# Two fp32 networks on one core: projections that end by token tiles, a reordered mixer, and two more places for experts' weights

## The chip, the cores and the metric

One core of a Trainium2 chip runs the whole program in one launch. The metric is device time in microseconds, from the first to the last instruction and what little lies around them, as the median of several runs. Lower is better.

## The reference

256 tokens of 1024 channels pass through two networks, all in fp32. The first has a mixer with dilated-window attention and a gated MLP, a layer of 16 experts, a mixer with two kinds of dense attention, a second layer of 16 experts, and a final norm. The second has four gated feed-forward stages, and between them a mixer of sliding-window attention beside a gated convolution with 31 taps, and a recurrent mixer. What the change touches, cut down:

```
for i in range(2):                               # first network
    x = x + mixer(rmsnorm(x, norm_mix[i]))       # ends with  cat @ w_out
    x = x + ec_moe(rmsnorm(x, norm_ffn[i]))

def ec_moe(h, w_router, w_gate, w_up, w_down):   # each expert takes its 32 best tokens
    aff = softmax(h @ w_router)
    gates, idx = top_k(aff.T, 32)
    y = (silu(h[idx] @ w_gate) * (h[idx] @ w_up)) @ w_down
    return scatter_add(idx, y * gates)

def attn_conv_mixer(h):                          # second network, "even2"
    q, k, v, a, b = split(h @ w_in)
    attn = sliding_window_attention(q, k, v, sinks, rel_bias)
    c = silu(layernorm(causal_conv31(a * sigmoid(b))))
    return concat([attn, c]) @ w_out
```

## The kernel before

`x` stays in SBUF as two tiles of 128 tokens by 1024 channels (t = 0, 1). A product of the mixers and the feed-forward stages is made of three fp32r matmuls (`mm3`): high by high, low by high and high by low part (lines 435 to 437). The parts of a weight piece come from `split`: ScalarE writes `whi` (line 423), VectorE or GpSimd subtracts it and writes `wlo` (line 424). There are seven pairs of `whi` and `wlo`. The activations' parts are `hThi` and `hTlo`, those of a mixer's output `chi` and `clo`.

**Weights.** All large loads are issued on SP's queue in program order, in pieces of 1 MB (128 partitions by 2048), into a ring of six slots (line 393). The experts' weights are used as raw fp32 (lines 1305 and 1359). A layer has 64 pieces for gate and up (`bg`, `bu`) and 32 for down (`by`). Where each piece goes is told by a string, `PLAN`: `r` is a ring slot, `s` a pair of `whi` and `wlo`, `l` and `h` the space of `hTlo` and `hThi`, and a digit is a named place of 8 KB per partition. The first `AHEAD` pieces of a layer can be loaded during the mixer ahead of it (`early`, lines 1200 and 1210); the rest follow as TensorE gives space back (`more`). `grow` opens the places, some at the mixer's start (`feed`) and some at the layer's. Pieces behind the string's end go through the ring.

**The projection at the end of the first network's mixers.** `out_proj(late=True)` multiplies `chi`, `clo` by the output weights. The last rows of the sum are taken in four quarters of 256 columns (`mm4`, `last4`): each quarter ends with the addition to `x`, four transposes (`xTq`), the norm's gain on the way out of PSUM (`hTw`, lines 476 and 478), the squares for the norm, and one quarter later the router's matmuls for those channels (`lg`, line 1157). The layer of experts then forms the norm's factor from the running sum of squares and makes the softmax and the top 32.

**The even mixer of the second network.** `gated` makes the convolution's two inputs (`ba`), `taps` and `spectrum` its transform (`hw`, `sp`) and the products `yw` (lines 1638 to 1642), then six `pf` groups make q, k and v from pieces of 1024 columns. `scores` and `softmax` follow (lines 703 to 728), `back` transforms the convolution back (`yt`) and normalises it, `silu` transposes it (`ty`) and writes `sy`, whose parts are the last four rows of `chi`. `gqa_T` transposes the probabilities (`pt`), `pv` multiplies them by v (`po`). The output projection takes the rows of `chi` in the order 4, 5, 6, 7, 0, 1, 2, 3 (`acc`).

Each engine runs its instructions in the order in which they stand in its queue. Within that order the program, its pools and its priorities decide.

Of the kernel before, what the change touches and what calls it, by code (L numbers as in the profile page):

```python
# [9 lines left out]
F32 = mybir.dt.float32  # L10
F32R = mybir.dt.float32r
AF = mybir.ActivationFunctionType
ALU = mybir.AluOpType
# [3 lines left out]
P = 128  # L17
# [17 lines left out]
PLAN = "7ssslhrrrrrr012ssss3456" "7ssslhrrrrrrssss456"  # L35
AHEAD = 23
# [276 lines left out]
class Core:  # L313
# [170 lines left out]

    def squares(self, n):
# [6 lines left out]
    def running(self, sums, ss, n, eng=None):  # L492

        if n:
            (eng or self.nc.gpsimd).tensor_tensor(sums, ss[:, :, 0] if n == 1 else sums, ss[:, :, n], ALU.add)

    def squares4(self, n, eng=None):
# [8 lines left out]
        self.running(self.s2, self.ss, n, eng)  # L506
# [7 lines left out]
    def pow_rstd(self, ss, n, k, eps=EPS, eng=None):  # L514
# [4 lines left out]
        rs = self.wk.tile([P, k], F32, tag=f"rs{k}", name="rs", bufs=4)  # L519
# [78 lines left out]
    def out_proj(self, cat, name, order, eng=None, late=False):  # L598
# [9 lines left out]
        def mm4(i, t, n):  # L608
            k = order[i]

            self.mm3(acc[n][:, t * S:t * S + S], tuple(v[:, k, t * P:t * P + P] for v in cat),
                     tuple(u[:, S * n:S * n + S] for u in parts[i]), i + t == 0, i == KT - 1 and t == 1)

# [5 lines left out]
        def more(n):  # L619
            if not acc and late:  # L620
                acc.extend(self.bank("acc") for n in range(4))
# [5 lines left out]
        def some(m, ahead=0):  # L627
# [3 lines left out]
            for i in range(i0, done[0]):  # L631
                for t in range(NT):
                    for n in range(4 if late else 2):
                        (mm4 if late else mm)(i, t, n)
# [27 lines left out]

        def rest(n):
            raw.extend(self.load(w[:, CHUNK * n:CHUNK * n + CHUNK]))

        return some, last4 if late else last, rest
# [65 lines left out]
    def even1(self, wz, lead):  # L732
        nc, tc, A = self.nc, self.tc, self.A
        with ExitStack() as cx:
# [3 lines left out]
            self.feed(0, "7012", lead)  # L738
# [3 lines left out]
            router = self.router(0, h0)  # L742
# [95 lines left out]
            self.early("12")  # L838
# [1052 lines left out]
```

## Time and profile before

| | |
|---|---|
| median of 3 runs | 1615.41 us (1615.23 to 1615.72) |
| profiled execution | 1610.24 us, its span 1608.5 us |
| granted TensorE clock, mean over the span | 0.961 |
| TensorE busy | 1467.1 us |
| VectorE, ScalarE, GpSimd busy | 793.0, 644.4, 83.8 us |
| read from HBM | 397.29 MB, 248 GB/s over the span |

Stages in the profiled execution, in us from the span's start: first mixer to 126, layer 0 of experts to 345, second mixer to 438, layer 1 of experts to 658, then the second network, with its even mixer from 842 to 957. A window gives each engine's busy time in a stretch, so a stage's own limit is read from its own windows and not from the whole span. The granted clock is a share of 2.4 GHz: 1.00 is that level and 0.50 is 1.2 GHz.

### The profile page before, as it was taken

How to read it: one execution, taken by the hardware profiler on the slowest of the kernel's cores; microseconds unless marked ns; L12 is line 12 of the kernel's file. 1: busy time of each engine (PE TensorE's matmuls, PEld its weight loads, DVE VectorE, ACT ScalarE, POOL GpSimd, SP SyncE). 2: the span in 40 equal slices, each digit the busy share in tenths (PEclk: the TensorE clock that was granted, in tenths of full speed). 3: DMA queues.
4: the chain of work that ended last, by engine and by line, in shares of the span. 5: the costliest groups of instructions: out<-in, count | busy, mean ns of one | idle time of the engine just before them, and what ended most of it. 6: DMA issues, size and time to landing. Idle time of an engine off the chain costs nothing.

```text
span 1608.5 us, 24597 instructions
## 1 busy us (share of the span) xinstructions
PE 1467.1 (91%) x10220; PEld 1155.4 (72%) x10220; DVE 793.0 (49%) x1328; ACT 644.4 (40%) x1042; POOL 83.8 (5%) x108
## 2 busy tenths in 40 slices
PE   9997967888988677799999899999999999999998
PEld 7794303455842145599895679999999999899997
DVE  6753102248421013555454656555765559865554
ACT  5741101148311012444443544444554447754442
POOL 0000000020000001200001410000000000000000
PEclk9998969999989799899999999999999999999999
DMA  9768999994799999856531535555555554555530
GB/s 364 303 247 334 416 419 420 417 386 152 277 389 417 419 414 382 349 181 218 198 131 54 209 108 208 183 185 186 179 184 185 187 186 142 209 181 183 186 130 26
DMA packets 60815, 399.94 MB, mean 249 GB/s; under 512 B 6808, under 2 KB 7200, under 8 KB 17312
## 3 DMA queue, kind: packets, MB, share of 16 engines
q1 hardware_dynamic: 59584, 394.03, 64.6%
q0 software_dynamic: 1120, 4.35, 0.8%
q8 instruction: 80, 1.31, 0.3%
q14 instruction: 31, 0.25, 0.0%
HBM read 397.29 MB, written 1.06 MB: 248 GB/s over the span
## 4 chain that ended last, share of the span: by engine, by line
PE 61%; issue 6%; DMA 5%; DVE 3%; ACT 2%; POOL 0%; POOLq 0%; DVEq 0%; ACTq 0%
PE acc L435 6%; PE acc L437 6%; PE acc L436 6%; PE bg L436 6%; PE bg L435 5%; PE bg L437 5%; PE bu L436 5%; PE bu L437 5%; PE bu L435 5%; DMA w<-in_m_gu_dram 3%; DMA w<-in_m_d_dram 2%; PE by L1359 1%; PE bu L1305 1%; PE bg L1305 1%; PE xs L1288 1%
## 5 line engine op out<-in xcount | busy, mean ns | idle before, releaser
L424 DVE TENSOR_TENSOR wlo<-w,whi 128x1024 fp32r<-128x1024 f32 x349 | 431.1, 1244 | 284.7 <-ACT whi L423 284.3
L423 ACT CAST whi<-w 128x1024 fp32r<-128x1024 f32 x357 | 369.8, 1046 | 461.6 <-PE acc L437 145.4
L435 PE MATMUL bg<-hThi,whi 128*128 128x256 f32 x752 | 212.8, 284 | 2.8 <-ACT hThi L481 2.4
L436 PE MATMUL bg<-hTlo,whi 128*128 128x256 f32 x752 | 211.6, 282 | 4.1 <-DVE hTlo L482 4.1
L437 PE MATMUL bg<-hThi,wlo 128*128 128x256 f32 x752 | 211.5, 281 | 0.0
L436 PE MATMUL bu<-hTlo,whi 128*128 128x256 f32 x656 | 184.4, 281 | 0.0
L437 PE MATMUL bu<-hThi,wlo 128*128 128x256 f32 x656 | 184.3, 281 | 0.0
L435 PE MATMUL bu<-hThi,whi 128*128 128x256 f32 x656 | 184.2, 281 | 0.0
L436 PEld LDWEIGHTS bg<-hTlo,whi 128*128 128x128 f32 x752 | 142.2, 189 | 7.5 <-DVE hTlo L482 5.8
L435 PEld LDWEIGHTS bg<-hThi,whi 128*128 128x128 f32 x752 | 141.8, 189 | 7.0 <-ACT hThi L481 3.9
L435 PE MATMUL acc<-whi,gh 128*128 128x512 f32 x352 | 139.7, 397 | 4.9 <-ACT gh L430 4.9
L437 PEld LDWEIGHTS bg<-hThi,wlo 128*128 128x128 f32 x752 | 142.2, 189 | 0.0
L436 PE MATMUL acc<-wlo,gh 128*128 128x512 f32 x352 | 139.9, 397 | 0.0
L437 PE MATMUL acc<-whi,gl 128*128 128x512 f32 x352 | 139.8, 397 | 0.0
L437 PEld LDWEIGHTS bu<-hThi,wlo 128*128 128x128 f32 x656 | 124.0, 189 | 0.0
L435 PEld LDWEIGHTS bu<-hThi,whi 128*128 128x128 f32 x656 | 124.0, 189 | 0.0
L436 PEld LDWEIGHTS bu<-hTlo,whi 128*128 128x128 f32 x656 | 123.8, 189 | 0.0
L435 PEld LDWEIGHTS acc<-whi,gh 128*128 128x128 f32 x352 | 66.6, 189 | 19.1 <-ACT gh L430 5.1
L437 PEld LDWEIGHTS acc<-whi,gl 128*128 128x128 f32 x352 | 66.4, 189 | 15.9 <-DVE gl L431 0.6
L1359 PE MATMUL by<-w,aT 128*32 128x256 f32 x1024 | 68.1, 391 | 10.4 <-DMA w<-in_m_d_dram 7.2
L436 PEld LDWEIGHTS acc<-wlo,gh 128*128 128x128 f32 x352 | 66.6, 189 | 14.0
L1338 DVE SCALAR_TENSOR_TENSOR hid<-bu,rsl,hid 128x512 f32<-128x512 f32 x8 | 6.0, 750 | 126.2 <-PE bu L1305 118.1
(407 smaller groups left out, 2284.1 us busy)
## 6 DMA issues: line engine op xcount, KB each, us to landing
w<-in_f_gu_dram SPq DMA_DIRECT2D x84, 1024.0 KB, 5.1
w<-in_m_gu_dram SPq DMA_DIRECT2D x68, 1024.0 KB, 13.3
w<-in_m_d_dram SPq DMA_DIRECT2D x64, 1024.0 KB, 11.7
w<-in_f_d_dram SPq DMA_DIRECT2D x40, 1024.0 KB, 5.1
wx<-in_m_gu_dram SPq DMA_DIRECT2D x32, 1024.0 KB, 9.9
wx<-in_m_gu_dram SPq DMA_DIRECT2D x56, 512.0 KB, 6.7
w<-in_e_out_dram SPq DMA_DIRECT2D x8, 1024.0 KB, 5.3
w<-in_o_out_dram SPq DMA_DIRECT2D x8, 1024.0 KB, 5.0
```

Of the source, the lines that this page charges most:

```text
L423: pin(nc.scalar.copy(hi[:, i:n], w[:, o + i:o + n]))
L424: pin((eng or nc.vector).tensor_sub(lo[:, i:n], w[:, o + i:o + n], hi[:, i:n].bitcast(F32)))
L435: mm(out, a[0], b[0], start=start, stop=False)
L436: mm(out, a[0], b[1], start=False, stop=False)
L437: mm(out, a[1], b[0], start=False, stop=stop)
L1288: nc.tensor.matmul(b[:, :n], self.x[:, t, k * P:k * P + P], ohf[:, t, q0 * P:q1 * P], start=t == 0, stop=t == NT - 1)
L1305: nc.tensor.matmul(b[32 * j:32 * j + 32], xs[q][:, k, 32 * j:32 * j + 32], w[j // 2][:, j % 2 * 512:j % 2 * 512 + 512], start=k == 0, stop ...
L1338: nc.vector.scalar_tensor_tensor(a, bu, rsl[:, q:q + 1], a, op0=ALU.mult, op1=ALU.mult)
L1359: nc.tensor.matmul(b[32 * j:32 * j + 32, o:o + S], aT[:, q, f, 32 * j:32 * j + 32], w[i][:, j * S:j * S + S], start=f == 0, stop=f == 3)
```

## The change

The output projections of the first network's mixers end by four tiles of 128 tokens by 512 columns (`tiles`), with the router's matmuls one tile behind. The transposed `x` goes to the router without the gain (`xTt`), and the gain is multiplied into the router's weights once. The squares are taken per tile and added up in `moe`. Two places, 8 and 9, are added: 8 is loaded in the mixers, 9 is opened at the start of a layer. Their space comes from the scratch for DMA descriptors of GpSimd's queue, set to 1 KB per partition, and from small tiles of `moe` that now share space; the load of `back` for the relative bias is cut into four. In the even mixer of the second network the first pair of q, k, v weights is split ahead of the gate, `pf` of piece 0 goes ahead of the transform, and the probabilities of the first tokens are transposed and multiplied by v around the second `back`, ahead of `silu`.

```diff
-PLAN = "7ssslhrrrrrr012ssss3456" "7ssslhrrrrrrssss456"
-AHEAD = 23
+PLAN = "7ssslhrrrrrr012ssss345689" "7ssslhrrrrrrssss45689"
+AHEAD = 25
+SCRATCH = 1024
...
+    def xTt(self, t, n):
+
+        b = self.bank("tp")
+        for k in range(4):
+            o = (4 * n + k) * P
+            self.nc.tensor.transpose(b[:, k * P:k * P + P], self.x[:, t, o:o + P], self.id)
+        bv = b.rearrange("p (k s) -> p k s", k=4)
+        h = self.hT[0][:, 4 * n:4 * n + 4, t * P:t * P + P]
+        self.nc.scalar.copy(h[:, :2], bv[:, :2])
+        self.nc.vector.tensor_copy(h[:, 2:], bv[:, 2:])
...
-        def last4(hook):
-
-            more(KT - len(parts))
-            for n in range(4):
-                for i in range(done[0], KT):
-                    for t in range(NT):
-                        mm4(i, t, n)
-                if n:
-                    hook(n - 1)
-                xs = self.x[:, :, S * n:S * n + S]
-                nc.vector.tensor_tensor(xs, xs, acc[n].rearrange("p (t c) -> p t c", t=NT), ALU.add)
-                self.room()
-                self.xTq(n)
-                self.squares4(n, nc.vector)
-            hook(3)
...
+        def tiles(hook):
+
+            more(KT - len(parts))
+            self.room()
+            self.ss = self.wk.tile([P, NT, 2], F32, tag="ss", name="ss")
+            todo = []
+            for n in range(2):
+                for t in range(NT):
+                    for i in range(done[0], KT):
+                        mm(i, t, n)
+                    if todo:
+                        hook(*todo.pop())
+                    xs = self.x[:, t, n * 512:n * 512 + 512]
+                    nc.vector.tensor_add(xs, xs, acc[t][n])
+                    self.xTt(t, n)
+                    self.square(xs, self.ss[:, t, n:n + 1], 1 - n)
+                    todo.append((t, n))
+            hook(*todo.pop())
...
-            self.feed(0, "7012", lead)
+            self.feed(0, "70128", lead)
...
-            self.early("12")
+            self.early("128")
...
-            self.feed(1, "70", lead)
+            self.feed(1, "708", lead)
...
-            self.early("70sss")
+            self.early("708sss")
...
-    def router(self, l, pool):
+    def router(self, l, pool, gain):
...
+        nc.vector.tensor_tensor(wr, wr, gain[:, :, None].to_broadcast([P, KT, NE]), ALU.mult)
+
+        def step(t, n):
...
-            self.grow("456" if l == 0 else "3456", cx)
+            self.grow("4569" if l == 0 else "34569", cx)
...
-            nc.vector.tensor_scalar(ms, self.s2, 1.0 / D, EPS, op0=ALU.mult, op1=ALU.add)
+            nc.vector.tensor_tensor(ms, self.ss[:, :, 0], self.ss[:, :, 1], ALU.add)
+            nc.vector.tensor_scalar(ms, ms, 1.0 / D, EPS, op0=ALU.mult, op1=ALU.add)
...
+                ws.extend(self.split(self.load(A["e2_in"][0])))
                 rs, _ = self.rstd()
...
-            def qkv(i, ws):
+            def qkv(i):
+                if i == len(ws):
+                    ws.extend(self.split(self.load(A["e2_in"][i // 2])))
...
             gated()
             taps()
+            qkv(0)
             y = spectrum()
-            for i in range(0, 6, 2):
-                ws = self.split(self.load(A["e2_in"][i // 2]))
-                qkv(i, ws)
-                qkv(i + 1, ws)
+            for i in range(1, 6):
+                qkv(i)
...
             p0 = scores(0, 0)
             back(y, 0)
             p1 = scores(1, 0)
+            p0 = self.gqa_T(1, p0)
             back(y, 1)
+            pv(0, p0)
             p1.update(scores(1, 2))
             silu()
-            pv(0, self.gqa_T(1, p0))
             some(3)
...
-                nc.gpsimd.dma_start(back, bass.AP(tensor=d.tensor, offset=d.offset, ap=[[1, P], [384, 8], [1, S]]))
+                for h in range(0, 8, 2):
+                    nc.gpsimd.dma_start(back[:, h:h + 2], bass.AP(tensor=d.tensor, offset=d.offset + 384 * h,
+                                                                  ap=[[1, P], [384, 2], [1, S]]))
...
-    nc = _bacc.Bacc("TRN2", target_bir_lowering=False, num_devices=1)
+    nc = _bacc.Bacc("TRN2", target_bir_lowering=False, num_devices=1, dynamic_dma_scratch_size=SCRATCH)
```

The string decides what SP issues. Its queue around the start of layer 0, before: the eight half pieces of the last `s` pairs, the places that the layer opens, and what follows (`wx` is a piece outside the ring, `w` one in it).

```order
L1200 DMA wx<-in_m_gu_dram 128x1024 x8
L1210 DMA wx<-in_m_gu_dram 128x2048 x4
L1200 DMA wx<-in_m_gu_dram 128x1024 x6
L1210 DMA wx<-in_m_gu_dram 128x2048 x2
L393 DMA w<-in_m_gu_dram 128x2048 x6
L1200 DMA wx<-in_m_gu_dram 128x1024 x8
L1210 DMA wx<-in_m_gu_dram 128x2048 x3
```

And in the changed kernel:

```order
L1208 DMA wx<-in_m_gu_dram 128x1024 x8
L1218 DMA wx<-in_m_gu_dram 128x2048 x5
L1208 DMA wx<-in_m_gu_dram 128x1024 x6
L1218 DMA wx<-in_m_gu_dram 128x2048 x2
L394 DMA w<-in_m_gu_dram 128x2048 x6
L1208 DMA wx<-in_m_gu_dram 128x1024 x8
L1218 DMA wx<-in_m_gu_dram 128x2048 x5
```

One more place is issued at the layer's start (five instead of four), two more in the second turn (five instead of three), and four ring pieces fewer follow. Place 8 stands further ahead, in the first mixer, behind two other places.

VectorE in the even mixer of the second network, from the gate to the second `pf`, before: `glu` is the gate, `yw` and `u` are the transform's products, `qT` the finished queries.

```order
L424 TENSOR_TENSOR wlo<-w,whi 128x1024
L1618 SCALAR_TENSOR_TENSOR glu<-ba,rs,glu 128x512 x2
L402 COPY hw<-hw 96x512 x2
L1638 TENSOR_TENSOR yw<-sp,hw 96x512 x2
L1639 TENSOR_TENSOR u<-sp,hw 96x512 x2
L1640 TENSOR_TENSOR yw<-yw,u 96x512 x2
L1642 TENSOR_TENSOR yw<-sp,hw 96x512 x2
L424 TENSOR_TENSOR wlo<-w,whi 128x1024 x3
L1679 TENSOR_TENSOR qT<-pf,rrow 128x256
L424 TENSOR_TENSOR wlo<-w,whi 128x1024 x2
L1679 TENSOR_TENSOR qT<-pf,rrow 128x256
```

And in the changed kernel:

```order
L425 TENSOR_TENSOR wlo<-w,whi 128x1024 x3
L1629 SCALAR_TENSOR_TENSOR glu<-ba,rs,glu 128x512 x2
L403 COPY hw<-hw 96x512 x2
L1692 TENSOR_TENSOR qT<-pf,rrow 128x256
L1649 TENSOR_TENSOR yw<-sp,hw 96x512 x2
L1650 TENSOR_TENSOR u<-sp,hw 96x512 x2
L1651 TENSOR_TENSOR yw<-yw,u 96x512 x2
L1653 TENSOR_TENSOR yw<-sp,hw 96x512 x2
L425 TENSOR_TENSOR wlo<-w,whi 128x1024
L1692 TENSOR_TENSOR qT<-pf,rrow 128x256
```

Two `wlo` more stand ahead of `glu`, the first `qT` ahead of `yw`, and one `wlo` instead of three behind `yw`.

ScalarE at the end of that mixer's softmax, before: `p` and `st` are the probabilities and their sums, `sy` the silu of the convolution.

```order
L400 COPY p<-pt 128x512
L708 ACTIVATE st<-st 128x2
L718 ACTIVATE p,st<-p,st 128x256 x2
L708 ACTIVATE st<-st 128x2
L718 ACTIVATE p,st<-p,st 128x256
L728 ACTIVATE p<-p,st 128x256
L718 ACTIVATE p,st<-p,st 128x256
L1670 ACT_TABLE_LOAD
L1670 ACTIVATE sy<-ty,pc_e_6580 128x256
L728 ACTIVATE p<-p,st 128x256
L430 CAST chi<-sy 128x256
L1670 ACTIVATE sy<-ty,pc_e_6580 128x256 x2
```

And in the changed kernel:

```order
L431 CAST chi<-po 128x4x128
L1681 ACT_TABLE_LOAD
L1681 ACTIVATE sy<-ty,pc_e_6361 128x256
L715 ACT_TABLE_LOAD
L715 ACTIVATE st<-st 128x2
L725 ACTIVATE p,st<-p,st 128x256 x2
L715 ACTIVATE st<-st 128x2
L725 ACTIVATE p,st<-p,st 128x256
L735 ACTIVATE p<-p,st 128x256
L725 ACTIVATE p,st<-p,st 128x256
L431 CAST chi<-sy 128x256
L1681 ACT_TABLE_LOAD
```

The first `sy` now stands ahead of the last four exps (`p,st<-p,st`), with a table load of its own on either side, and its `chi` behind them.

## Rows read from the trace of the kernel before

**Rows 1.** The page: busy us, share of the span; DMA's tenths in 40 slices.
```profile
PE 1467.1 (91%) x10220; PEld 1155.4 (72%) x10220; DVE 793.0 (49%) x1328; ACT 644.4 (40%) x1042; POOL 83.8 (5%) x108
...
DMA  9768999994799999856531535555555554555530
```

**Rows 2.** Windows of layer 0: from:to, length, each engine's busy us (instructions), PEclk, DMA share, GB/s.
```profile
39.00:45.00 6.00, 5.27 (x39) 4.30 (x38) 5.37 (x20) 5.71 (x7) 0.00 (x0) 1.00 0.21 49
135.00:141.00 6.00, 6.00 (x26) 2.80 (x27) 1.31 (x4) 0.37 (x1) 0.00 (x0) 0.50 0.46 146
141.00:340.00 199.00, 162.27 (x1284) 70.52 (x1282) 28.63 (x55) 26.39 (x51) 3.40 (x5) 0.91 1.01 415
```

**Rows 3.** Chain of waits, 480 to 600 us: start us, us, what.
```profile
499.50 18.76 DMA w<-in_m_gu_dram
...
564.45 13.78 DMA w<-in_m_d_dram
```

**Rows 4.** Windows around layer 1, columns as in group 2.
```profile
385.00:391.00 6.00, 4.83 (x32) 2.61 (x28) 4.58 (x11) 5.64 (x15) 0.00 (x0) 1.00 0.03 11
451.00:454.00 3.00, 3.00 (x28) 1.11 (x24) 0.35 (x1) 0.00 (x0) 0.00 (x0) 0.87 0.69 199
...
605.00:630.00 25.00, 19.98 (x198) 12.91 (x198) 6.32 (x9) 5.42 (x13) 3.60 (x3) 1.00 0.96 390
```

**Rows 5.** Waits of TensorE, 20 to 60 us: us in total, times, longest.
```profile
PE sc L817 <- ACT qkT L807: 0.7, 1, 0.7
```

**Rows 6.** Timeline of SP's queue at the start of layer 0: start us, us, what.
```profile
126.11 13.11 SPq L1210 DMA_DIRECT2D wx<-in_m_gu_dram  x4
```

**Rows 7.** Timeline of TensorE in the even mixer's projections.
```profile
902.44 0.28 PE L436 MATMUL pf<-hTlo,whi 128*128 128x256 f32 x1
902.56 0.28 PE L437 MATMUL pf<-hThi,wlo 128*128 128x256 f32 x1
```

**Rows 8.** Timeline of TensorE, end of the first mixer; idle time and releaser in brackets.
```profile
124.89 1.12 PE L1157 MATMUL lg<-pc_wr,hTw 128*128 128x16 f32 x8 [0.58 <-DVE hTw L478]
```

**Rows 9.** Timeline of TensorE in the even mixer of the second network.
```profile
885.73 0.58 PE L437 MATMUL pf<-hThi,wlo 128*128 128x256 f32 x1 [4.47 <-DVE wlo L424]
...
910.58 3.70 PE L1652 MATMUL yt<-yw,pc_e 96*128 96x512 f32 x8
...
919.17 1.79 PE L1140 MATMUL po<-p,v 128*64 128x512 f32 x2 [2.37 <-DVE p L402]
...
923.87 0.50 PE L435 MATMUL acc<-whi,chi 128*128 128x512 f32 x1 [0.45 <-ACT chi L430]
```

**Rows 10.** Timeline of VectorE there.
```profile
883.27 1.27 DVE L1642 TENSOR_TENSOR yw<-sp,hw 96x512 f32<-96x512 f32 x2
884.47 3.48 DVE L424 TENSOR_TENSOR wlo<-w,whi 128x1024 fp32r<-128x1024 f32 x3
...
890.28 4.56 DVE L424 TENSOR_TENSOR wlo<-w,whi 128x1024 fp32r<-128x1024 f32 x2
...
919.03 0.54 DVE L1658 TENSOR_SCALAR yt<-yt,ls,rs 128x512 f32<-128x512 f32 x1
```

**Rows 11.** Window behind the wait of `pf`, columns as in group 2.
```profile
885.00:888.00 3.00, 2.27 (x10) 2.27 (x11) 2.94 (x3) 0.00 (x0) 0.00 (x0) 0.54 0.75 262
```

**Rows 12.** Timeline of ScalarE there.
```profile
914.04 0.49 ACT L718 ACTIVATE p<-p,st 128x256 f32<-128x256 f32 x1
...
914.53 0.49 ACT L718 ACTIVATE p<-p,st 128x256 f32<-128x256 f32 x1
...
921.27 1.28 ACT L1670 ACT_TABLE_LOAD   x1
922.57 0.56 ACT L1670 ACTIVATE sy<-ty,pc_e 128x256 f32<-128x256 f32 x1
...
923.43 0.39 ACT L430 CAST chi<-sy 128x256 fp32r<-128x256 f32 x1
```

**Rows 13.** DMA issues: name, queue, count, KB each, median us to landing.
```profile
row_fn<-in_row_fn_dram POOLq DMA_DIRECT2D x1, 512.0 KB, 8.8
```

More of the change, by code (lines that the diff above doesn't have):

```diff
@@ L518, in pow_rstd @@
         (eng or nc.vector).tensor_scalar(ms, ss, 1.0 / n, eps, op0=ALU.mult, op1=ALU.add)
-        rs = self.wk.tile([P, k], F32, tag=f"rs{k}", name="rs", bufs=4)
+        rs = self.wk.tile([P, k], F32, tag=f"rs{k}", name="rs", bufs=4 if k == NT else 2)
         nc.gpsimd.tensor_tensor(rs, ms, self.mhalf[:, :k], ALU.pow)
@@ L606, in out_proj @@
         done = [0]
[L608 to L612, printed above, removed]
         def mm(i, t, n):
@@ L619, in more @@
         def more(n):
-            if not acc and late:
-                acc.extend(self.bank("acc") for n in range(4))
             if not acc:
@@ L661, in last @@
                 self.xT(n)
+        def tiles(hook):
[3 more added lines that the diff above has]
+            todo = []
+            for n in range(2):
+                for t in range(NT):
+                    for i in range(done[0], KT):
+                        mm(i, t, n)
+                    if todo:
[6 more added lines that the diff above has]
+            hook(*todo.pop())
         def rest(n):
             raw.extend(self.load(w[:, CHUNK * n:CHUNK * n + CHUNK]))
-        return some, last4 if late else last, rest
+        return some, tiles if late else last, rest
     def rope(self, v, r, co, si, pool):
@@ L741, in even1 @@
             self.small("e1", hp, nc.sync)
-            router = self.router(0, h0)
+            router = self.router(0, h0, self.c("g_ffn0"))
             tab = self.c("ropeA").rearrange("p (c t r) -> p c t r", c=2, t=NT)
@@ L900, in odd1 @@
             self.small("o1", hp)
-            router = self.router(1, h0)
+            router = self.router(1, h0, self.c("g_ffn1"))
             rs, ms = self.rstd()
@@ L1149, in router @@
         wr = self.c(f"wr{l}").rearrange("p (k e) -> p k e", k=KT)
-        def step(n):
-            if n == 0:
+        nc.vector.tensor_tensor(wr, wr, gain[:, :, None].to_broadcast([P, KT, NE]), ALU.mult)
+        def step(t, n):
+            if t + n == 0:
                 self.lgs = self.bank("lg")[:, :NT * NE].rearrange("p (t e) -> p t e", t=NT)
-            for k in range(2 * n, 2 * n + 2):
-                for t in range(NT):
-                    nc.tensor.matmul(self.lgs[:, t], self.hT[0][:, k, t * P:t * P + P], wr[:, k], start=k + t == 0,
-                                     stop=k + t == KT)
+            for k in range(4 * n, 4 * n + 4):
+                nc.tensor.matmul(self.lgs[:, t], self.hT[0][:, k, t * P:t * P + P], wr[:, k], start=t + k == 0,
+                                 stop=t + k == KT)
         return step
@@ L1245, in moe @@
             nc.gpsimd.tensor_tensor(rs, ms, self.mhalf[:, :NT], ALU.pow)
-            st = hp.tile([P, 4, NT], F32, name="rst")
+            wab = hp.tile([P, 2, S], F32, name="wab")
+            st = wab[:, 1, :4 * NT].rearrange("p (i t) -> p i t", i=4)
             nc.vector.tensor_reduce(st[:, 0], lgs, AX.X, ALU.max)
@@ L1256, in moe @@
                 nc.tensor.transpose(b[:NE, t * P:t * P + P], aff[:, t], self.id)
-            wa = hp.tile([NE, S], F32, name="wa")
-            wb = hp.tile([NE, S], F32, name="wb")
-            m8 = hp.tile([NE, 8], F32, name="m8")
+            wa, wb = wab[:NE, 0], wab[:NE, 1]
+            oh = hp.tile([P, NT, NE, CAP], F32, name="oh")
+            m8 = oh[:NE, 0, 0, :8]
             src = b[:NE, :S]
@@ L1273, in moe @@
             key = b[:, :NT * NE].rearrange("p (t e) -> p t e", t=NT)
-            oh = hp.tile([P, NT, NE, CAP], F32, name="oh")
             for e in (slice(0, 4), slice(4, NE)):
@@ L1291, in gather @@
                     self.scaled(xs[q][:, k], b[:, (q - q0) * P:(q - q0) * P + P], g[:, k:k + 1])
-            gt = hp.tile([P, 4], F32, name="gt")
-            rsl = hp.tile([P, 4], F32, name="rsl")
+            gr = hp.tile([P, 2, 4], F32, name="gr")
+            gt, rsl = gr[:, 0], gr[:, 1]
             ohT = None
@@ L1600, in even2 @@
             rs = row = None
+            ws = []
             def gated():
```

14 lines of the change are left out of this document (6 added, 8 removed).

## Prediction

> **What bounds the kernel now.** I read the page's busy times and slices first, then the windows and the waits of the stages that the diff touches. Over the whole span TensorE is busy 91% [rows 1], but that is an average over stages with different limits. The line of DMA tenths holds 9 in two stretches: those are the two layers of experts. In the first of them, 141 to 340 us, the DMA engines are full (share 1.01, 415 GB/s) while TensorE is busy 162 of 199 us at a mean clock of 0.91 [rows 2]. A 1 MB piece, 1,048,576 bytes, takes 1,048,576 / 415,000 = 2.53 us there. The chain of waits of layer 1 says the same: its long links are transfers of experts' weights, 18.76 us at 499.50 and 13.78 us at 564.45, with single matmul groups of about 1 us between them [rows 3]. So the end of the up projections, and of the first down group, goes by bytes that are still to come when the layer starts. From the second down group on, no such link stands; DMA has gaps (share 0.96 in 605 to 630, [rows 4]) and TensorE's own work sets a steady pace, so an earlier start is carried through unchanged. In the second network DMA's tenths are 5 or 6 and less [rows 1]; there TensorE sets the pace, so what the even mixer there wins or loses is carried to the end as well.
>
> **Two places more.** A place is 1 MB that can be loaded before the layer needs it; it is worth 2.53 us if its transfer goes into time when DMA is idle, and nothing if DMA is busy then. Place 8 goes out behind the first two places of the even mixer, ahead of most weights of that mixer's own projections. In 39 to 45 us DMA's share is 0.21, which leaves 4.7 us free [rows 2]. The queries and keys behind it come 2.5 us later; between 20 and 60 us the longest wait of TensorE is 0.7 us, for ScalarE and not for a transfer [rows 5], so I take that delay as covered (if not, it costs at most those 2.5 us). In layer 1, 385 to 391 us has a share of 0.03, 5.8 us free [rows 4]. So place 8 gives -2.5 us in each layer. Place 9 opens when the layer begins. In layer 0 SP issues four L1210 loads from 126.11 and stands at the fourth until 139 us, since that one needs place 7 back from TensorE [rows 6]; meanwhile 135 to 141 us has a share of 0.46, 3.2 us free [rows 2]. One more megabyte fits: -2.5 us. In layer 1 the same spot, 451 to 454, has a share of 0.69, 0.9 us free [rows 4]: -0.9 us. Together -5.0 and -3.4, **-8.4 us**. The bounds: with nothing from place 9, -5.0; more than 10.1 (four full megabytes) is not to be had.
>
> **Tiles instead of quarters.** An accumulation over 512 columns costs what two over 256 do: the split matmuls run at 0.12 us per 256 columns, from one start to the next [rows 7], and both forms stream the same columns. What counts is the tail behind the last accumulation. Now the last router matmuls start at 124.89, after waiting 0.58 us for the scaled copy `hTw`, whose two halves run one after the other on VectorE and ScalarE [rows 8]. Afterwards the last tile has as many transposes (4), as many router matmuls (4) and two copies one after the other, with a 512-wide square ahead of ScalarE's copy instead of a 256-wide one. The gain's multiplication moves to one VectorE operation per layer, in front where VectorE has room. I take 0, with -0.3 to +0.3 us per layer.
>
> **The even mixer, first half.** TensorE ends `sp`, starts `pf` on the two high parts that are ready, and then stands 4.47 us until 885.73, for `wlo` from VectorE [rows 9]. VectorE is late because the products `yw` come first in its queue: the last pair starts at 883.27 and only then, at 884.47, the subtraction that TensorE waits for [rows 10]. The change splits the first pair before `glu`, where both engines idle, puts `pf` of piece 0 ahead of `sp` and lets piece 1 run while VectorE forms `yw`. The 48 matmuls of those two pieces take 48 x 0.12 = 5.8 us [rows 7]; four of them ran before the stall already. Counted from the end of `sp`, the next `wlo` still comes 4.9 us later; `sp` ends 2.9 us later, and at the resumption 48 matmuls fewer are left, so the gain is 5.8 - 2.9 = 2.9 us. The stall also cost speed: the granted clock in 885 to 888 is 0.54 [rows 11], 1.2 GHz for most of it, with TensorE idle before; I put -0.5 us on a shorter stall. Against that, GpSimd's subtractions for `e2_out` begin earlier, beside VectorE's `yw`; two VectorE splits beside GpSimd took 4.56 us where three alone took 3.48 [rows 10]: up to +1.1 us for the one that TensorE waits for, of which I take 0.5. Sum **-2.9 us**, bounds -4.5 and -0.5.
>
> **The even mixer, second half.** Here I read a loss. Before, both `yt` groups are issued without a wait (the second at 910.58, 3.70 us), then TensorE stands 2.37 us before `po` [rows 9]. Afterwards most of the second `yt` stands behind the eight transposes `pt`, and these need the normalised `p`: ScalarE is through with its second pair at 914.04, where the next exp starts [rows 12]. With one exp more ahead of that pair it is 914.5; four matmuls of `yt` and the transposes between them (3.70 + 0.3) then end at about 918.5, 4.2 us later than before. `po` follows without its stall, but the layer norm behind `yt` (VectorE, GpSimd, ScalarE, GpSimd, VectorE, in all some 3.5 us) ends near 922, where it ended at 919.57 [rows 10]. That puts the first `sy` at about 922.9, instead of 922.57. What is queued behind it is the larger part. Before, one table load stands ahead of all four `sy`, and `chi` for the first matmul begins 0.86 us after `sy`, at 923.43 [rows 12]. Afterwards ScalarE has `sy`, a table load, two sink exps, four row exps and one scaling, and only then that `chi`: 0.5 + 1.28 + 0.2 + 4 x 0.49 + 0.4 = 4.3 us after `sy` began (the exps go 0.49 apart [rows 12]). `chi` would begin at 927.2 and TensorE start `acc` at 927.7, where it started at 923.87 [rows 9]: **+3.8 us**, in which TensorE idles, since the order of the projection's rows is fixed and nothing else may go first. The second extra table load stands ahead of the next `sy`, whose matmuls come 2.8 us later; it just fits. Bounds +0.5 (`sy` comes so early that the exps behind it are over in time) and +5.5 (the clock falls in the idle time, as above).
>
> Here a page of the Trainium skill (ScalarE: Activation LUTs, section "What ACT_TABLE_LOAD costs") speaks against the change: it counts a drain of about 1380 ns beside the 1283 ns of each switch. The trace agrees with the load (1.28 us) but not with a drain: the next `sy` starts at 922.57, 1.30 us after the load began [rows 12]. By the page's figure the two switches would cost 5.3 us instead of 2.6 (an estimate), and the whole gain would be smaller by up to 2.7 us.
>
> **The sum.** -8.4 + 0 - 2.9 + 3.8 = **-7.5 us**. The profiled execution took 1610.24 us, 1.74 more than its span, so it would take 1602.7; the median of the three timed runs is 5.17 us above the profiled one, so the forecast is 1615.4 - 7.5 = **1607.9 us**.
>
> **The rivals.** (a) The second half costs little, +0.5: then -10.8, or 1604.6. For it: the scores of the second half may be ready before `sy`, and 2.37 us of stall vanish. Against it: ScalarE works strictly in its order, and in that order `chi` is behind the exps. (b) Place 9 gives nothing, because what comes out of the freed wait is a transfer that TensorE needs less, or place 8 delays the even mixers' own weights and gives back its 2.5 us in one layer and more: -5.0 for the places, -4.1 in all, or 1611.3. (c) The places do nothing at all: TensorE at the lower clock in 135 to 141 (0.50, [rows 2]) would set the pace of the layer's start, and the transfers would only wait longer. Then 0 - 2.9 + 3.8 = +0.9, or 1616.3, no change. Against it stands the full share for 199 us. (d) Slower: 1 KB of scratch for the DMAs that GpSimd issues. Place: the end of layer 1, where GpSimd issues `row_fn` and `pc_t` in the middle of the chain that forms the norm's factor. If the memory holds fewer descriptors than one such DMA needs together with the one before it, GpSimd stands until the earlier has landed, 8.8 us for `row_fn` [rows 13] and about as much for the other. If both block, the sum is -7.5 + 17.6, or 1625.5; it decides from 7.5 + 3.2 = 10.7 us of blocking on. Against it: most DMAs of that queue come alone, tens of us apart. The Trainium skill (SBUF — State Buffer, section "SBUF size: 192, 224, or 256?") counts 16 KiB for this scratch and calls it the ring of descriptors; it does not say what a smaller one costs, and no run here shows it. (e) Each table switch costs as much again as the load itself: 1.3 us more ahead of the first `chi`, and 1.3 more ahead of the second, which then comes too late for TensorE: -7.5 + 2.6 = -4.9, or 1610.5. The rows speak against it; it is what the page on the tables would make of this change.
>
> **The numbers.** A change under 0.2%, 3.2 us, can't be told from none here. Chances: forecast (1606 to 1610) 0.42, (a) 0.25, (b) 0.15, (c) 0.08, (d) 0.07, (e) 0.03. Faster by over 3.2 us: the forecast, (a), (e) and three quarters of (b), 0.81; within: the rest of (b) and (c), 0.12; slower 0.07. The range begins at (a) with -4.5 in the first half and -0.6 in the two tails, -8.4 - 4.5 + 0.5 - 0.6 = -13.0, or 1602.4, and ends at (b) with +5.5 in the second half, -5.0 - 2.9 + 5.5 = -2.4, or 1613.0.
>
> **What would show it.** Right: in 135 to 141 us a share near 0.9; first down groups of both layers ending 5.0 and 8.4 us earlier; `pf` resuming with a wait under 2.5 us; `acc` of the even mixer waiting 4 to 5 us for `chi`, with two more table loads. Wrong: DMA still idle before 141, up projections that wait for something other than a transfer, GpSimd's DMA issues that take microseconds, or an `acc` that starts without a wait.

## The result, and the profile after

The changed kernel takes 1593.22 us (median of 4 runs, 1592.43 to 1598.0), the kernel before 1615.32 us in the same comparison: a ratio of 0.987, 95% interval 0.985 to 0.989. That is 22.1 us faster. The forecast was 7.5 us, and the time lies below its range. On two other chips the same two kernels differed by 18.8 us (ratios 0.9891 and 0.9892). The profiled execution took 1593.49 us, its span 1591.4.

The page's busy times and DMA's tenths, to be held against [rows 1]:

```profile
PE 1456.4 (92%) x10028; PEld 1140.9 (72%) x10028; DVE 789.0 (50%) x1318; ACT 645.6 (41%) x1036; POOL 87.0 (5%) x111
...
DMA  9779999994799999855522435555455553555530
```

TensorE was busy 1467.1 us before, and is 10.7 us less now. The two stretches of nines stay: what bounds the layers of experts has not changed.

**The start of layer 0.** SP's queue, which answers to [rows 6]:

```profile
124.07 12.85 SPq L1218 DMA_DIRECT2D wx<-in_m_gu_dram  x5
137.41 3.43 SPq L1208 DMA_DIRECT2D wx<-in_m_gu_dram  x6
```

Five loads stand where four stood, and the next six are issued at 137.41. Windows of the layer, columns as in [rows 2]:

```profile
39.00:45.00 6.00, 5.27 (x36) 4.17 (x35) 5.77 (x23) 5.72 (x9) 0.00 (x0) 1.00 0.25 61
133.00:136.00 3.00, 3.00 (x16) 2.03 (x20) 1.28 (x3) 0.37 (x1) 0.00 (x0) 0.50 0.88 371
136.00:139.00 3.00, 3.00 (x28) 1.06 (x24) 0.00 (x0) 0.37 (x1) 0.00 (x0) 0.98 0.48 115
139.00:332.00 193.00, 157.74 (x1275) 70.30 (x1266) 29.11 (x56) 26.96 (x51) 3.40 (x5) 0.92 1.01 418
```

The full stretch of the layer's loads, to 332 us now and to 340 before, is as full as it was (share 1.01) and begins at 139 instead of 141; of the hole ahead of it the first half is filled. In 39 to 45 us, where the prediction wanted place 8 to go, the share is 0.25 and was 0.21: the megabyte is not there (see *no_places*). The chain of waits in layer 1 (start us, us, what), beside [rows 3], still has the experts' weights as its long links:

```profile
494.82 19.80 DMA w<-in_m_gu_dram
...
552.10 12.21 DMA w<-in_m_d_dram
```

**The even mixer of the second network.** Timeline of TensorE, beside [rows 9]; in brackets the idle time and who ended it:

```profile
863.42 5.31 PE L1645 MATMUL sp<-glu,pc_e 128*96 128x512 f32 x12
872.66 0.39 PE L438 MATMUL pf<-hThi,wlo 128*128 128x256 f32 x1 [0.67 <-DVE wlo L425]
891.80 0.73 PE L1135 MATMUL pt<-pc_id,p 128*128 128x128 f32 x4 [1.28 <-ACT p L735]
894.44 0.69 PE L1135 MATMUL pt<-pc_id,p 128*128 128x128 f32 x2 [1.91 <-ACT p L735]
910.35 0.79 PE L436 MATMUL acc<-whi,chi 128*128 128x512 f32 x1 [4.71 <-ACT chi L431]
```

The stall of 4.47 us before `pf` is down to 0.67. At the end `acc` waits 4.71 us for `chi`. ScalarE's timeline there, beside [rows 12]:

```profile
903.99 1.28 ACT L1681 ACT_TABLE_LOAD   x1
905.45 0.56 ACT L1681 ACTIVATE sy<-ty,pc_e 128x256 f32<-128x256 f32 x1 [0.18 <-PE ty L1678]
906.03 1.28 ACT L715 ACT_TABLE_LOAD   x1
907.33 0.20 ACT L715 ACTIVATE st<-st 128x2 f32<-128x2 f32 x1
...
909.90 0.39 ACT L431 CAST chi<-sy 128x256 fp32r<-128x256 f32 x1
910.31 1.28 ACT L1681 ACT_TABLE_LOAD   x1
```

From the start of the first `sy` at 905.45 to the start of its `chi` at 909.90 it does what the prediction listed, in 4.45 us (the prediction: 4.3).

**What nothing had announced.** In the gated feed-forward stages of the second network, which the diff does not touch, TensorE runs faster. VectorE writes `gl` once per chunk there; the grouped lines of the two stages behind the even mixer give the first and the last start (`x22` is the count; then ns min/median/max, first and last start). Before:

```profile
L431 DVE TENSOR_TENSOR gl<-act,gh x22: 683/684/687, 971.4 to 1321.8; 128x512 fp32r<-128x512 f32 x22
```

After:

```profile
L432 DVE TENSOR_TENSOR gl<-act,gh x22: 684/684/686, 959.5 to 1306.6; 128x512 fp32r<-128x512 f32 x22
```

The same 22 instructions span 350.4 us before and 347.1 after. The 256-wide matmuls of gate and up follow each other more closely. TensorE's timeline, before:

```profile
1067.86 0.28 PE L435 MATMUL bg<-hThi,whi 128*128 128x256 f32 x1
...
1070.94 0.28 PE L437 MATMUL bu<-hThi,wlo 128*128 128x256 f32 x1
```

The same 27 matmuls after:

```profile
1055.24 0.28 PE L436 MATMUL bg<-hThi,whi 128*128 128x256 f32 x1
...
1058.27 0.28 PE L438 MATMUL bu<-hThi,wlo 128*128 128x256 f32 x1
```

26 steps take 3.08 us before, 3.03 after: 0.1185 and 0.1165 us each (this is the pitch, from one start to the next), both at a granted clock of 1.00. The 512-wide matmuls beside them (`acc`) keep 0.233. Over all four stages the spans of `gl` add up to 643.5 us before and 637.3 after.

### The profile page after: what moved, and what is told of

The parts are those of the page before. It is cut to its first block, busy times and chain, and to the rows that moved or that the text cites. A ratio compares the mean times of both kernels' runs of the same rounds, so it can differ in the third digit from the quotient of the medians.

```text
span 1591.4 us, 24189 instructions
## 1 busy us (share of the span) xinstructions
PE 1456.4 (92%) x10028; PEld 1140.9 (72%) x10028; DVE 789.0 (50%) x1318; ACT 645.6 (41%) x1036; POOL 87.0 (5%) x111
## 3 DMA queue, kind: packets, MB, share of 16 engines
q8 instruction: 78, 1.28, 0.3%
## 4 chain that ended last, share of the span: by engine, by line
PE 60%; DMA 5%; DVE 3%; ACT 3%; POOL 1%; issue 1%; POOLq 0%; DVEq 0%; ACTq 0%; SPq 0%
PE acc L436 6%; PE acc L438 6%; PE acc L437 6%; PE bg L436 6%; PE bg L437 6%; PE bg L438 5%; PE bu L437 5%; PE bu L438 5%; PE bu L436 5%; DMA w<-in_m_gu_dram 3%; PE by L1368 2%; DMA wx<-in_m_gu_dram 1%; DMA w<-in_m_d_dram 1%; PE xs L1297 1%; PE pf L438 1%; PE pf L436 1%
## 5 line engine op out<-in xcount | busy, mean ns | idle before, releaser
L411 DVE TENSOR_SCALAR hid<-by,gr 128x256 f32<-128x256 f32 x16 | 7.7, 484 | 119.3 <-PE by L1368 119.3
```

The lines of the kernel that those rows point to most:

```text
L411: self.nc.vector.tensor_scalar(out, in_, s, None, op0=ALU.mult)
```

## The experiments

*scratch*, *shift*, *pad* and *old_softmax* ran on one chip (the kernel before: 1613.92 us), *no_places*, *old_tiles*, *old_even2* and *again* on another (1612.67), *best*, *after_there*, *gap64* and *gap256* on a third (1612.9). Ratios are to the kernel before on the same chip, with 95% intervals.

**Where the close pitch comes from.** Three things could do it: the small scratch, where the tiles lie, or the chip of the day. The place hangs on one line of the diff that the section on the change cuts away:

```diff
-        rs = self.wk.tile([P, k], F32, tag=f"rs{k}", name="rs", bufs=4)
+        rs = self.wk.tile([P, k], F32, tag=f"rs{k}", name="rs", bufs=4 if k == NT else 2)
```

These are the norms' small tiles, not those of `moe` that the section on the change names. The line takes 128 bytes per partition out of a pool that lies between `hThi`, `hTlo` and the weights' parts, and so moves everything behind that pool. In the programs as built, `hThi` begins at 960 modulo 1024 bytes in all kernels here; every `whi` and `wlo` begins at 800 modulo 1024 before, at 672 after.

*shift*: the kernel before with that line alone. 

> The kernel before with one change: the small tiles rs of the norms have two buffers instead of four where they are not of width 2, which takes 128 bytes per partition out of the pool that lies between the activations' parts and the weights' parts. No instruction is added or removed. Theory A (place of the weights relative to the activations): 1606 to 1609, pitch of the 256-wide matmuls in the feed-forward stages 0.1166. Theory B (scratch): 1615, pitch 0.1186. Theory C: 1615, any pitch.

Measured: 1601.38 us (1598.32 to 1607.65), ratio 0.9933 [0.9911, 0.9956].

```profile
L431 DVE TENSOR_TENSOR gl<-act,gh x22: 683/683/686, 966.9 to 1314.0; 128x512 fp32r<-128x512 f32 x22
```

347.1 us, as after. The ratio makes 10.8 us of one line about small tiles (0.67% of 1613.92), more than its theory expected (1606 to 1609). Not all of that is pitch: of the 8.3 us between the two profiles, 5.4 lie in the four spans of `gl`, and in the even mixer the clock did not fall during `sp` as it had before (5.3 us there); other stages are up to 2 us longer.

*pad*: the changed kernel with the line as before. 

> The changed kernel with the buffers of rs back at four, which puts the weights' parts where they lay before relative to the activations' parts (128 bytes further up). Theory A: 1600 to 1602 instead of 1593, pitch 0.1186. Theories B and C: 1593, pitch 0.1166 (B) or any (C).

Measured: 1603.36 us (1598.67 to 1605.04), ratio 0.9934 [0.9911, 0.9957], against the changed kernel's 0.987 in the result and 0.9891 and 0.9892 in *again* and *after_there*: the line back as it was costs 0.4 to 0.6% of the time, 7 to 10 us. The same lines:

```profile
L432 DVE TENSOR_TENSOR gl<-act,gh x22: 683/684/687, 964.9 to 1315.3; 128x512 fp32r<-128x512 f32 x22
```

350.4 us, as before; over all four stages 644.0 us instead of the 637.3 of the profile after. The line alone decides the pitch. All fourteen profiles fall into two groups by the place of the weights' parts: with 672 or 928 the four spans add up to 637.3 to 638.6 us, with 736 or 800 to 643.5 to 644.3. So the place is worth about 6 us in the feed-forward stages; what the medians and ratios show beyond that is not tied to the pitch.

*scratch*: the kernel before with 1 KB of scratch.

```diff
+                for h in range(0, 8, 2):
+                    nc.gpsimd.dma_start(back[:, h:h + 2], ...)
...
+    nc = _bacc.Bacc("TRN2", ..., dynamic_dma_scratch_size=1024)
```

> The kernel before with 1 KB of descriptor scratch and the load of back cut into four, nothing else; every tile moves down by 15,360 bytes per partition, the distances between tiles stay. Theory A (the weights' parts lie 128 bytes nearer to the activations' parts, which speeds up the 256-wide matmuls of the feed-forward stages from 0.1186 to 0.1166 us): no change, 1615, pitch 0.1186. Theory B (the smaller scratch itself, or the space it frees, does it): 1606 to 1609, pitch 0.1166. Theory C (the difference of pitch is one of executions or chips and not of the program): no change against the kernel before, any pitch. The rival of the forecast in which GpSimd blocks at small scratch: 1625, and DMA issues on GpSimd that last microseconds.

Measured: 1610.74 us (1606.42 to 1616.76), ratio 0.9983 [0.9964, 1.0003]: no change. The `gl` lines span 974.3 to 1324.7, 350.4 us. GpSimd issues its DMAs at the end of layer 1 without standing still, in 0.62 and 0.59 us here as in the kernel before. Its timeline in the changed kernel:

```profile
650.59 0.62 POOL L378 DMA_DIRECT2D row_fn<-in_row_fn_dram  x1
...
653.20 0.59 POOL L373 DMA_DIRECT2D pc_t<-in_pc_t_dram  x1
```

*gap64* and *gap256*: is it the distance, or the place in a grid? Both are the changed kernel without its two places, with an unused tile ahead of the weights' parts (64 or 256 bytes).

```diff
+        self.gap = self.wk.tile([P, 16], F32, name="gap", bufs=1)     # gap256: [P, 64]
```

> The changed kernel without its two places (so that there is room), with an unused 64 bytes per partition between the activations' parts and the weights' parts: the weights begin at 736 modulo 1024, between 672 (pitch of the 256-wide gate and up matmuls of the feed-forward stages 0.1166 us) and 800 (0.1186). Theory 1, any offset but the one at 672 costs: 0.1186. Theory 2, only the offset at 800, or one 128 bytes apart in some grid, costs: 0.1166. Between the two, a value of 0.1174 to 0.1178 would say that the cost grows with the offset. The two feed-forward stages behind the even mixer take 3.5 us more at the slow pitch.

> As the one with 64 bytes, but with 256 bytes: the weights begin at 928 modulo 1024, an even number of 128-byte steps from 672. Theory 1, only offsets modulo 256 matter: pitch 0.1166 as at 672. Theory 2, the distance between activations and weights as such matters, the further from 672 the worse: 0.1186 or above.

Grouped lines with 64 bytes, then with 256:

```profile
L433 DVE TENSOR_TENSOR gl<-act,gh x22: 682/684/686, 969.9 to 1320.2; 128x512 fp32r<-128x512 f32 x22
```

```profile
L433 DVE TENSOR_TENSOR gl<-act,gh x22: 682/684/685, 967.3 to 1314.3; 128x512 fp32r<-128x512 f32 x22
```

350.3 us with the weights at 736, 347.0 at 928. So 672 and 928 are fast, 736 and 800 slow: the pitch does not grow with the distance. Four offsets agree with a grid of 256 bytes, in which 672 and 928 are the same place. One run each (1608.69 and 1601.07 us); that the place in the grid is the cause, and not something else that moves along, such as the tiles behind the weights, is not separated.

**The places.** *no_places*: the changed kernel with the string, the orders and `AHEAD` of before.

```diff
-PLAN = "7ssslhrrrrrr012ssss345689" "7ssslhrrrrrrssss45689"
-AHEAD = 25
+PLAN = "7ssslhrrrrrr012ssss3456" "7ssslhrrrrrrssss456"
+AHEAD = 23
```

> The changed kernel without places 8 and 9 (the old string, 23 pieces early), all else as changed. If the places are worth what the forecast says (8.4 us): 1601 to 1602, the first down group of layer 0 about 5.0 us later and that of layer 1 another 3.4 us later than in the changed kernel. Rival (the layers gain from the earlier router, not from the places): under 1596.

Measured: 1604.36 us (1601.1 to 1606.48), ratio 0.9948 [0.9933, 0.9964]; the changed kernel on the same chip 1593.91. That is 10.5 us by medians, 9.2 by the ratios (0.9948 and 0.9891). The additions of the experts' results to `x`, grouped, of layers 0 and 1 without the places:

```profile
L1377 DVE TENSOR_TENSOR x<-x,sct x4: 686/687/689, 266.1 to 339.6; 128x512 f32<-128x512 f32 x4
...
L1377 DVE TENSOR_TENSOR x<-x,sct x4: 686/686/689, 578.3 to 652.6; 128x512 f32<-128x512 f32 x4
```

And with them:

```profile
L1377 DVE TENSOR_TENSOR x<-x,sct x4: 686/686/689, 260.8 to 333.0; 128x512 f32<-128x512 f32 x4
...
L1377 DVE TENSOR_TENSOR x<-x,sct x4: 686/689/689, 568.0 to 643.7; 128x512 f32<-128x512 f32 x4
```

The last router matmuls start at 123.11 without and 122.96 with the places in layer 0, at 433.42 and 426.55 in layer 1. From there to the first addition it is 143.01 against 137.85 us, and 144.88 against 141.46: 5.2 and 3.4 us. At the last addition, counted from the same matmuls, it is 6.5 and 2.0, 8.5 in all: from the first addition to the last a layer takes one of two times about 1.4 us apart (72.0 to 72.3 or 72.9 to 73.5, and 74.2 to 74.4 or 75.7 to 76.2, over the fourteen profiles), and why is open. Windows without the places:

```profile
133.00:136.00 3.00, 3.00 (x16) 2.12 (x20) 1.43 (x4) 0.37 (x1) 0.00 (x0) 0.50 0.16 66
136.00:139.00 3.00, 3.00 (x28) 0.99 (x24) 0.00 (x0) 0.37 (x1) 0.00 (x0) 0.94 0.44 85
```

The share in 133 to 136 is 0.16 without and 0.88 with place 9: its megabyte goes just there. Place 8 shows somewhere else than forecast. In 39 to 45 us the share is 0.21 without and 0.25 with it. SP issues it in a group of three at 9.71 us, into the full stretch up to 39 us; a load of the mixer's own weights moves back from 22.0 to 43.5 us, and what gets fuller is a later hole. Without the places, then in the changed kernel:

```profile
78.00:84.00 6.00, 6.00 (x47) 4.57 (x46) 5.42 (x14) 4.31 (x8) 0.00 (x0) 1.00 0.55 221
```

```profile
78.00:84.00 6.00, 6.00 (x48) 4.57 (x47) 5.31 (x14) 4.42 (x8) 0.00 (x0) 1.00 0.91 374
```

**Tiles or quarters.** *old_tiles*: the changed kernel with the old ends of the projections and the gain on the copies.

```diff
-        return some, tiles if late else last, rest
+        return some, last4 if late else last, rest
...
-        nc.vector.tensor_tensor(wr, wr, gain[:, :, None].to_broadcast([P, KT, NE]), ALU.mult)
```

> The changed kernel with the old ends of the two projections: quarters of 256 columns, the gain on the way out of PSUM, the running sum of squares. Forecast's term (the tiles are worth nothing, at most 0.3 us per layer): 1593 to 1594, router matmuls of both layers at most 0.3 us later. Rival (the tiles give what the mixers gained, 1.9 us in the first and 1.9 in the second): 1596 to 1597.

Measured: 1597.31 us (1592.06 to 1598.81), ratio 0.99 [0.9868, 0.9933], 3.4 us above the changed kernel on that chip; the intervals overlap. In the trace the last router matmuls start 1.88 us later in the first mixer, and from the last addition of layer 0 to the last router matmul the second mixer takes 96.74 us instead of 95.00, 1.74 more. The first part of the first mixer's accumulation on TensorE, in quarters:

```profile
92.31 0.39 PE L436 MATMUL acc<-whi,chi 128*128 128x256 f32 x1
...
109.68 1.91 PE L877 MATMUL pt<-pc_id,p 128*128 128x128 f32 x16
```

And in tiles:

```profile
91.54 0.50 PE L436 MATMUL acc<-whi,chi 128*128 128x512 f32 x1
...
107.99 1.25 PE L883 MATMUL pt<-pc_id,p 128*128 128x128 f32 x10
```

144 matmuls of 256 columns take 17.37 us (0.1206 each), 72 of 512 take 16.45 (0.2285 each): the same columns, 0.92 us less. From the last rows' first `acc` (113.40 and 111.71) to the last `lg` it is 11.44 and 11.25. The rest, 0.77 us, was there before the accumulation began (92.31 and 91.54): in this profile the granted clock fell early on (0.76 in 5 to 12 us, 1.00 in the profile after), as it did in five others of either form. In those six the accumulation begins at 91.97 to 92.47 us, in the eight others at 91.36 to 92.11. What does repeat is the accumulation: 17.37 or 17.38 us in all four profiles with quarters, 16.43 to 16.48 in all ten with tiles. Over all fourteen, the first mixer ends on average 1.1 us later with quarters (125.04 to 125.75 against 123.62 to 125.32), and the second takes 0.8 us more (96.3 to 96.7 against 94.9 to 95.6, and 97.5 and 97.8 in two). By the ratios, 0.9900 and 0.9891, the tiles are worth 1.5 us, with intervals that overlap almost wholly.

**The even mixer.** *old_even2*: the changed kernel with the whole mixer in the old order.

```diff
-            qkv(0)
             y = spectrum()
...
-            p0 = self.gqa_T(1, p0)
             back(y, 1)
-            pv(0, p0)
             p1.update(scores(1, 2))
             silu()
+            pv(0, self.gqa_T(1, p0))
```

> The changed kernel with the whole even mixer of the second network in its old order. Forecast's terms (first half -2.9, second +3.8): about 0.9 us faster than the changed kernel. Reading of the two traces (first half -7.0, second +8.4): 1.4 us faster. Rival (the low clock during hw and sp was chance in the kernel before, so the old first half costs only about 2): 6 us faster, 1587; then the transform of this kernel runs at a granted clock near 1.00.

Measured: 1593.95 us (1587.89 to 1597.89), ratio 0.9886 [0.985, 0.9922]; the changed kernel on that chip 1593.91. The two halves together are worth nothing that the medians show. But its four runs lie in two pairs, at 1587.89 and 1590.63 and at 1597.28 and 1597.89. The profiled run is the one of 1590.63, and there the clock stays at 1.00 during `sp`, which is what the rival named: from the last `ba` to the first addition to `x` it takes 73.11 us, where *again* takes 80.34.

*old_softmax*: only the second half in the old order. 

> The changed kernel with the second half of the even mixer in its old order: both yt groups first, then the last scores, silu, and only then the transposes and the product with v of the first tokens. From the trace of the changed kernel: the new order lost 6.6 us from the transposes of v to the first acc and 1.8 us more up to the addition to x. Theory (ScalarE's order with its table loads and the transposes ahead of yt cost this): about 1585, acc waits under 1 us for chi, two table loads fewer. Rival (the loss is the price of the faster first half, whose work only moves): 1592 to 1594.

Measured: **1587.53 us** (1586.05 to 1590.43), ratio 0.9846 [0.9822, 0.987]. Faster than both kernels. TensorE's timeline there:

```profile
899.91 1.97 PE L1147 MATMUL po<-p,v 128*64 128x512 f32 x2 [2.54 <-DVE p L403]
904.62 0.50 PE L436 MATMUL acc<-whi,chi 128*128 128x512 f32 x1 [0.61 <-ACT chi L431]
```

The old stall before `po` is back and `acc` starts 5.7 us earlier than in the changed kernel.

*best* and *after_there*: the same version again, beside the changed kernel on a third chip. 

> The changed kernel with the old second half of the even mixer (the second back transform, the last scores and silu ahead of the first transposed probabilities), now beside the changed kernel on one chip. Theory (the new second half costs 8 us, because the first chi stands behind a table load, the sink exps and the row exps): the projection's first matmul starts 6 to 7 us earlier than in the changed kernel, the first addition to x some 8 us earlier, and the time is 6 to 9 us below the changed kernel's on this chip. Rival (that loss is made good later, and the earlier difference was one of chips): within 2 us of it.

> The changed kernel once more, on the same chip as the version with the old second half. Both theories expect what it measured before: a ratio of 0.987 to 0.989 to the kernel before; it is here so that the other version has a neighbour on its own chip.

Measured: 1587.71 us (1586.39 to 1591.62), ratio 0.9854 [0.9819, 0.989], against 1594.08 (1591.97 to 1598.34), 0.9892 [0.9861, 0.9923]: 6.4 us. In this execution of the changed kernel (*after_there*) the clock stayed at 1.00 in the softmax, where it had fallen in the profile after (next section):

```profile
895.00:900.00 5.00, 3.09 (x12) 1.59 (x11) 3.75 (x20) 4.98 (x20) 0.63 (x1) 1.00 0.00 0
900.00:905.00 5.00, 4.29 (x23) 1.91 (x21) 2.04 (x7) 2.91 (x5) 0.79 (x2) 1.00 0.53 180
```

*again*: the changed kernel as neighbour of the second four. 

> The changed kernel once more, for what its stages differ by from one execution to the next. Feed-forward stages within 0.2 us of the first trace; the two layers of experts within 1.5 us each; 1592 to 1594.

 Measured: 1593.91 us (1593.18 to 1595.71), ratio 0.9891 [0.9868, 0.9914]. The four spans of `gl` are each within 0.2 us of the first trace, and both layers within 0.5.

## Why the prediction was wrong

The step that failed is the sum itself: **-8.4 + 0 - 2.9 + 3.8 has no term for where tiles lie.** The change was read as edits of order and space. That one line of it moves the weights' parts by 128 bytes, and that this changes the pitch of matmuls in stages that the change does not touch, was put at nothing without a word. It measured 5.4 us (*shift*) to 6.7 us (*pad*) in the four feed-forward stages.

By stage, the span of the profiled execution went from 1608.5 to 1591.4 us, 17.1 less: the two layers of experts -8.5 (forecast -8.4), the even mixer of the second network +1.2 (forecast +0.9), the two mixers with the new ends -3.2 (forecast 0), the feed-forward stages -6.2 (no term), all else -0.4. The other 5 us up to 22.1 come from the scatter of the runs: the profiled execution of before lies 5.1 us under its median, which the forecast carried over unchanged, and that of after lies at its own. Where the slower runs of before lose those 5 us no profile shows; on the two other chips, with 18.8, that part is smaller.

By ratios to the kernel before on the same chip: places -9.2, offset -10.8 (*shift*) or -6.9 (*pad* against 0.9891), tiles -1.5, even mixer +0.8. Together -20.7 or -16.8, where the ratio 0.9891 makes -17.6.

**Places, -8.4 (-5.0 and -3.4).** Right in mechanism and in size: -5.2 and -3.4 at the first additions, -8.5 in all at the last ones, -9.2 by ratios. Full DMA ahead of the first addition, a hole before it, and a megabyte that goes into a hole. For place 9 in layer 0 it is the hole that was named. For place 8 in the first mixer it is not: 39 to 45 us stayed as empty as it was (0.25), and 78 to 84 filled up (0.55 to 0.91), so that its 2.5 us came out right is in part luck. Rivals (b) and (c) fall. The queries and keys behind place 8 cost nothing that shows: the first mixer's last router matmuls start at 122.96 with it and at 123.11 without.

**Tiles, 0 per layer.** The tail was judged rightly (11.44 against 11.25), the accumulation wrongly. "An accumulation over 512 columns costs what two over 256 do" took one pitch, 0.12, for both forms; 256-wide matmuls ran at 0.1206 per 256 columns, 512-wide at 0.2285 / 2 = 0.1143. That is 0.9 us of the first part of a mixer's accumulation, in every profile. The mixers are 0.8 to 1.1 us shorter on average; more, as the medians of *old_tiles* would have it (3.4 for both), is not clear of the noise.

**Even mixer, first half, -2.9 (bounds -4.5 and -0.5).** From the last `ba` to the first `tv` (the transposes of v) it took 36.73 us before and takes 29.71: -7.0, beyond the bound. The order does what was said: VectorE's `yw` no longer stands ahead of the awaited `wlo`, and the wait is 0.67 us (0.6 to 2.1 in the ten profiles with this order). But most of the size is clock. Windows of `sp` before:

```profile
872.50:880.50 8.00, 8.00 (x14) 2.89 (x13) 2.67 (x5) 7.20 (x8) 0.66 (x1) 0.63 0.00 1
```

After:

```profile
863.40:868.20 4.80, 4.80 (x15) 1.87 (x13) 2.86 (x5) 1.92 (x3) 3.75 (x2) 1.00 0.01 2
```

In the first, TensorE was at 1.2 GHz for most of the time (0.63) and `sp` took 8.34 us; in the second at 2.4, 5.31. Where `sp` kept 1.00 in the old order, in *shift* and *old_even2*, the stretch from the last `ba` to the first `tv` took 31.60 and 30.85 us, and the wait for `wlo` was 2.73 instead of 4.47. The new order takes 29.5 to 31.1 in the ten profiled executions of kernels that have it. In *old_even2* and *old_softmax*, the old order and the new, the clock is 1.00 in the whole stretch:

```profile
859.08:889.93 30.85, 27.33 (x170) 20.81 (x168) 24.69 (x24) 14.04 (x16) 18.53 (x6) 1.00 0.36 126
```

```profile
855.47:884.99 29.52, 26.87 (x170) 20.73 (x169) 20.59 (x22) 11.42 (x13) 18.04 (x6) 1.00 0.27 96
```

That is 1.3 us. So the order by itself is worth 0 to 2 us, less than the 2.9 of the forecast, and about 5 us are what the clock took from the profiled execution of before. The prediction let that execution's `sp` and its wait stand as the cost of the old order. By medians the half is worth more, about 6.4 us: both halves together are 0.0, and the second alone loses that much. It fits that the old order meets the low clock more often: *scratch*, which has it too, ran `sp` at 0.77 and took 35.64 us, so that of four profiles with the old order two are slow here, and none of ten with the new. Why it does so stays open.

**Even mixer, second half, +3.8 (bounds +0.5 and +5.5).** The mechanism came out line by line: `sy`, a table load, the exps, the scaling, and only then `chi`, with `acc` waiting 4.71 us. From `tv` to `acc` it is 19.45 us before and 22.99 in *after_there*: +3.5, the forecast's size. But *after_there* is the exception. In the profile after it is 26.06, +6.6, with a fall of the clock while TensorE stood 1.28 and 1.91 us for `p`, and in the six other profiles with this order it is 24.7 to 26.1; all six with the old order have 19.45 to 19.63. Windows of the changed kernel, from the first `pt`, and from `acc`:

```profile
893.00:898.00 5.00, 3.56 (x8) 1.91 (x9) 3.25 (x16) 4.36 (x17) 0.63 (x1) 0.59 0.00 0
898.00:903.00 5.00, 5.00 (x14) 1.86 (x14) 0.70 (x2) 0.66 (x2) 0.22 (x1) 0.73 0.12 21
...
910.30:916.30 6.00, 5.95 (x18) 4.71 (x19) 1.90 (x6) 5.10 (x9) 0.00 (x0) 0.66 0.00 0
```

The last one is a price that the prediction left out of the sum, and had only as its upper bound: 4.71 us of idle time, then 0.66 at the start of the projection, another 1.8 us until its first addition to `x` (24.61 us instead of 22.80). All eight profiles with the new order have 24.1 to 25.5 here, but so have two of the six with the old one (*scratch* and *best*, 24.3 and 24.5). By the medians of *best* and *after_there* the half costs 6.4 us. Rival (a) falls.

**Scratch and table loads.** Rival (d) falls: GpSimd's issues take 0.6 us and *scratch* shows no change. Rival (e) falls: the first of the two added loads begins 0.02 us after `sy` ends (905.45 + 0.56 and 906.03), and the exps' first operation 1.30 us after the load does (906.03 to 907.33). The drain of about 1380 ns beside each load, in the Trainium skill (ScalarE: Activation LUTs, section "What ACT_TABLE_LOAD costs"), is not to be seen in this trace.

## What to carry to other kernels

Treat every edit of a buffer count as a move of all tiles behind it: before you credit the change, compare matmul pitches in stages that it does not touch. Read an operation's duration together with the granted clock of its window, and take a second execution before a stall or a long transform enters a sum. Where an order puts another function's work between a producer and its short consumer on ScalarE, count the whole queue to that consumer; and reverse such parts one at a time, since here one half hid what the other cost, and the version without the bad one, 1587.5 us, beats both kernels.

## What the runs showed of the hardware that was not expected

In the feed-forward stages, split matmuls of 128x256 that stream `hThi` and `hTlo` against the weights' parts follow each other on average 0.1167 or 0.1168 us apart with the weights' parts at 672 or 928 modulo 1024 bytes, and 0.1183 to 0.1185 at 736 or 800, with `hThi` at 960; 512-wide ones took 0.233 to 0.235 at all of these. Why is open. The 256-wide quarters of the first mixer (`acc`), which stream the weights' parts, took 17.38 us for 144 at 800 (before) and at 672 (*shift*) alike. Waits of TensorE of 1.28 and 1.91 us in one mixer came with a granted clock of 0.59 and 0.73 in one execution of the changed kernel, and of 1.00 in another; behind the wait of 4.7 us all eight profiles with it show 0.50 to 0.76 over the next 6 us.
